# Moving four small pieces of work in a two-layer hybrid backbone: seam weights, s2 parts, last splits, context split

## The chip, the cores and the metric

One core of one Trainium2 chip runs the whole program. The metric is the time of one execution in microseconds on the device; the kernel before is given by the median of three runs. A profile was taken of one more execution. In it PE is TensorE's matmuls, PEld its weight loads, DVE is VectorE, ACT ScalarE, POOL GpSimd, and SP is SyncE, whose queue issues nearly all transfers.

## The reference

Two layers work on 1024 latent tokens and 256 context tokens of width 1024, all in float32. Only the second half of a layer matters here, the gated MLP:

```python
def conv_ffn(h, lp):
    up = h @ lp['w_up']
    gate, val = jnp.split(up, 2, axis=-1)
    gate = dwconv(gate, lp['ffn_conv_w'], lp['ffn_conv_b'], (FFN_CONV - 1) // 2)
    return (jax.nn.silu(gate) * val) @ lp['w_down']
...
    x = x + g2 * conv_ffn(modulate(rms_norm(x, lp['norm2_gain']), sh2, sc2), lp)
    if ctx_out:
        ...
        xc = xc + g2c * conv_ffn(modulate(rms_norm(xc, lp['norm2_gain']), sh2c, sc2c), lp)
```

`w_up` is 1024 x 5632 and `w_down` 2816 x 1024. `ctx_out` holds in layer 0 alone, so layer 1 has no context in its MLP.

## The kernel before, in words

**Splits.** Every float32 matmul operand is split into a rounded high part and the rest: `hi` (line 183) is a copy on ACT, `lo` (line 186) a subtraction on DVE or POOL. A product is then three matmuls, high by high, high by rest, rest by high. `weight` (line 189) loads 512 KB into a `raw` buffer (there are two), splits it on ACT and POOL, and gives a tile of the tag `wt` (there are six).

**The stages of a layer.** Phase A projects, phase B has the three head groups, `phase_c` the output projection and the MLP. In `phase_c`, `norm_ops` (line 1179) forms the operands of the up product, `up(f)` runs 22 slices of 128 columns, and each slice goes to DRAM (`ud`). `down_steps` (line 1279) takes slices 0 to 19 in five steps of four, and `down` (line 1715) takes the last two slices with weights of their own. In layer 0 that last part is a function `tail`, kept and called at the beginning of layer 1 (line 278): it stands inside a block that the framework plans as a whole with a model of time, together with phase A of layer 1. This place is called the seam.

**Seven products instead of eight.** Both big products use the Winograd form: sums of operand quarters (s1 to s4 of the activations, t1 to t4 of the weights) and seven block products. In `norm_ops` s2 = v22 - bias - v11 and s4 = v12 + bias - s2, each in four parts kk of 128 x 512; part 0 goes through a tile of its own (`sx`) and is split last. `product` (line 1546) runs kk = 0, 1, 2, 3, three matmuls each. In the last layer the order of the products of the first four slices is t1 s1, t3 s3, t4 a22, t2 s2, b22 s4. The t4 product adds into the bank of t3, after DVE has added that bank into `vb`.

**The down steps.** A step has seven products (p1 to p7), and in layer 0 a context-only factor c. `prep(g)` (line 1350) splits the two factors of product g and forms the sums of product g + 1 on POOL (`ensure`), two products ahead of use; four buffer pairs go round. `split_ctx` (line 1326) splits four context pieces of 128 x 256 on ACT and POOL; the first context product comes after the step's second product. Every product ends in DVE additions to the residual, which release its PSUM banks.

**What sets the order.** Operations are traced in the program's order, but each engine's queue is then ordered by the framework, which goes by priority and a model of when inputs are ready. So an operation that seems ready early can stand in its engine's queue in front of work that was traced before it. Inside the block of line 278 the model of time is a finer one. Engines run their queues in order.

```python
        with self.tc.block(schedule_with_timeline_sim=True):
            if l:
                self.tail()
            self.phase_a()
```

Of the kernel before, what the change touches and what calls it, by code (L numbers as in the profile page):

```python
# [11 lines left out]
F32 = mybir.dt.float32  # L12
F32R = mybir.dt.float32r
# [157 lines left out]
class Build:  # L171
# [9 lines left out]


    def hi(self, out, in_):
        self.nc.scalar.activation(out, in_, AF.Copy)  # L184

    def lo(self, out, in_, hi, eng=None):
        (eng or self.nc.vector).tensor_tensor(out, in_, hi.bitcast(F32), ALU.subtract)  # L187

    def weight(self, src, n=1024):
        nc = self.nc  # L190
# [988 lines left out]
    def norm_ops(self, xt, am, bm, accs, f_tile, bank, ops, early, outs):  # L1179
# [13 lines left out]
        def unit(name, t, c=0):  # L1193
            p = t[:, c:c + 512], t[:, c + 512:c + 1024]
            ops[name].append(p)
            return p

        def split(p, v, eng):
            self.hi(p[0], v)
            self.lo(p[1], v, p[0], eng)  # L1200
# [51 lines left out]
        for kk in range(4):  # L1252
            s3 = v21[kk]
            nc.vector.tensor_tensor(s3, v11[kk], s3, ALU.subtract)
            split(unit("s3", (wa, wb)[kk // 2], 1024 * (kk % 2)), s3, nc.vector)
        ops["s2"].append(None)
        ops["s4"].append(None)
        for kk in range(4):
# [20 lines left out]
    def down_steps(self, xt, f_tile, bank):  # L1279
# [41 lines left out]
        def load_ctx(s):  # L1321
            if not self.last:
                for i in range(4):
                    nc.sync.dma_start(ctx[i], self.ud[4 * s + i, :, NLAT:])

        def split_ctx():
            if not self.last:
                for v, (hi, lo) in zip(ctx, cs):
                    self.hi(hi, v)
                    self.lo(lo, v, hi, nc.gpsimd)  # L1330
# [19 lines left out]
        def prep(g):  # L1350
            if g >= len(seq):
                return
            s, p = seq[g]
            an, bn = ops[p][:2]
            i = g % 4
            ah, al = (t[:, :W] for t in ra[i])
            bh, bl = rb[i][:, :W], rb[i][:, W:]
            factors(g)
            if an:
                self.hi(ah, st[an])  # L1360
                self.lo(al, st[an], ah)
            self.hi(bh, st[bn])
            self.lo(bl, st[bn], bh, nc.gpsimd if g % 2 else nc.vector)
            made[s, p] = ah, al, bh, bl
            factors(g + 1)
            if s + 1 < steps:
                left = set()
                for q in [q for t, q in seq[g + 1:] if t == s]:
                    for n in ops[q][:2]:
                        left.add(n)  # L1370
                for n, (u, v, _) in sums.items():
                    if done.get(n, -1) < s:
                        left |= {u, v}
                names = [n for n in raw if n not in left and loaded[n] == s]
                for n in names:
                    loaded[n] = s + 1
                load(s + 1, *names)
# [67 lines left out]
        load_ctx(0)  # L1445
        prep(0)
        prep(1)
        split_ctx()
        if steps > 1:
            load_ctx(1)  # L1450
        g = 0
        for s in range(steps):
            mine = [p for t, p in seq if t == s]
            for i, p in enumerate(mine):
                prep(g + 2)
                g += 1
                if p != "c":
                    product(s, p)
                if not self.last:

                    for q in {1: ("p1",), len(mine) - 1: ("c",)}.get(i, ()) + ((p,) if p in ("p2", "p3") else ()):
                        context(s, q)
                if s + 1 == steps:
                    for n in {"p2": ("x12",), "p5": ("x22",), "p7": ("x21",)}.get(p, ()):
                        spread(n)
                    for n in {"p2": ("x11",), "p7": ("x22",), "p3": ("x12",), "p4": ("x21",)}.get(p, ()):
                        store(n)
            if s + 1 < steps:
                split_ctx()
                if s + 2 < steps:  # L1470
                    load_ctx(s + 2)
# [3 lines left out]
    def phase_c(self):  # L1475
# [3 lines left out]
        with ExitStack() as st:  # L1479
# [59 lines left out]
            def split(v, name, eng=None):  # L1539
                r = next(ring)  # L1540
                h, lo = r[:, 0:512], r[:, 512:1024]
                self.hi(h, v[name])
                self.lo(lo, v[name], h, eng or (nc.gpsimd if name in ("t3", "b11", "b21") else nc.vector))
                v[name] = h, lo

            def product(ps, w, a, new, wts):
                (wh, wl), aa = wts[w], ops[a]
                for kk in range(4):
                    s = slice(P * kk, P * kk + P)
                    h, lo = aa[kk]  # L1550
                    nc.tensor.matmul(ps, wh[:, s], h, start=new and kk == 0, stop=False, skip_group_check=not new)  # L1551
                    nc.tensor.matmul(ps, wh[:, s], lo, start=False, stop=False, skip_group_check=not new)  # L1552
                    nc.tensor.matmul(ps, wl[:, s], h, start=False, stop=kk == 3, skip_group_check=not new)  # L1553

            def context(ps, w, new, wts):
                hh, hl = hc
# [151 lines left out]
            def load_u(f):  # L1708
                h, lo = self.h_tile("uh"), self.h_tile("ul")
                nc.sync.dma_start(lo[:, :n_tok].bitcast(F32), self.ud[f][:, :n_tok])  # L1710
                self.hi(h[:, :n_tok], lo[:, :n_tok].bitcast(F32))
                self.lo(lo[:, :n_tok], lo[:, :n_tok].bitcast(F32), h[:, :n_tok])
                return h, lo

            def down(fs, us, ds, end=False):
# [34 lines left out]
            if self.last:  # L1750
                ds = weights()
                down([NF - 2, NF - 1], [load_u(f) for f in (NF - 2, NF - 1)], ds)
            else:
                us = []
                for f in (NF - 2, NF - 1):
                    h, lo = f_tile("uh", F32R), f_tile("ul", F32R)
                    nc.sync.dma_start(lo.bitcast(F32), self.ud[f])
                    self.hi(h, lo.bitcast(F32))
                    self.lo(lo, lo.bitcast(F32), h)
                    us.append((h, lo))  # L1760
                stack = st.pop_all()

                def tail():
                    mods, self.mods = self.mods, self.modl[l]
                    ds = weights()
                    for j in range(KC):
                        xt[j] = self.x_tile(f"xt{j}") if j < KC - 1 else self.z_tile("xt7")[:, :T]
                    for o, n in CH:
                        for j in range(KC):
                            nc.sync.dma_start(xt[j][:, o:o + n], self.xp[j][:, o:o + n])  # L1770
                    down([NF - 2, NF - 1], us, ds, True)
                    self.mods = mods
                    stack.close()
                    del self.s5

                self.tail = tail
                return
# [26 lines left out]
```

## Time and profile before

| | us |
|---|---|
| three runs | 3067.39, 3073.74, 3075.61 |
| median | 3073.74 |
| profiled execution, its own time | 3074.54 |
| its span, first to last instruction | 3072.8 |
| PE busy | 2836.2 (92%) |
| DVE busy | 2070.9 (67%) |
| POOL busy | 1520.2 (49%) |
| ACT busy | 1468.6 (48%) |

The span is the profiled execution without what lies around the first and last instruction. Layer 0 runs to about 1661, its last two down slices and layer 1 follow. A busy share is a mean over stages with different limits; the waits of PE and the timeline around them tell more.

### The profile page before, as it was taken

To read this page: it belongs to the slowest core of one execution; us is meant where nothing else is said; L and a number is where in the kernel's file an instruction comes from. 1 tells how busy PE (TensorE), PEld (TensorE's weight loads), DVE (VectorE), ACT (ScalarE), POOL (GpSimd) and SP (SyncE) were. 2 spreads that over 40 slices of the span, in tenths; PEclk is the share of its full clock that TensorE was granted. 3 is DMA by queue.
4 is the path that set the end of the run, shared out by engine and by line. 5 is a ranking of instruction groups with operands and counts; after the bars stand their busy time and mean duration, and the time that the engine had idled before them with its cause. 6 is when DMAs were issued, how large, how long until landed. Compare 5 with 4: busy or idle time off the path is not lost. (4 is left out here: it accounts for less than half of the span.)

```text
span 3072.8 us, 40965 instructions
## 1 busy us (share of the span) xinstructions
PE 2836.2 (92%) x15146; PEld 2308.8 (75%) x15146; DVE 2070.9 (67%) x2879; ACT 1468.6 (48%) x2450; POOL 1520.2 (49%) x1011
## 2 busy tenths in 40 slices
PE   6999898999899999998988899898999799999898
PEld 4798665678688888886877788666777678887776
DVE  6956656884854444457887985757885755556997
ACT  5544467784443433342332554567883444444331
POOL 4746412323554444448561765512323576665971
PEclk9999999999899999998999999999999999999999
DMA  7232627664122111143215331545533122224322
GB/s 254 83 85 82 173 61 248 185 196 172 38 81 76 67 68 67 67 182 113 83 56 192 112 109 52 145 109 168 130 121 131 55 89 83 83 83 158 123 83 83
DMA packets 208280, 349.25 MB, mean 114 GB/s; under 512 B 32720, under 2 KB 112336, under 8 KB 208080
## 3 DMA queue, kind: packets, MB, share of 16 engines
q1 hardware_dynamic: 203472, 331.69, 33.3%
q0 software_dynamic: 4608, 14.95, 2.2%
q8 instruction: 119, 1.95, 0.3%
q14 instruction: 81, 0.66, 0.1%
HBM read 257.19 MB, written 89.39 MB: 113 GB/s over the span
## 5 line engine op out<-in xcount | busy, mean ns | idle before, releaser
L184 ACT ACTIVATE w_r<-w_raw 128x512 fp32r<-128x512 f32 x338 | 212.7, 631 | 451.4 <-PE u_ps L1552 279.7
L1524 POOL TENSOR_TENSOR w_raw<-w_raw 128x512 f32<-128x512 f32 x176 | 249.9, 1425 | 229.3 <-DVE w_r L187 108.5
L187 DVE TENSOR_TENSOR w_r<-w_raw,w_r 128x512 fp32r<-128x512 f32 x206 | 151.3, 737 | 250.2 <-ACT w_r L184 250.1
L1551 PE MATMUL u_ps<-a,w_r 128*128 128x512 f32 x704 | 278.6, 396 | 5.1 <-DVE vb L1639 4.0
L1552 PE MATMUL u_ps<-a,w_r 128*128 128x512 f32 x704 | 277.5, 394 | 1.4 <-DVE a L187 1.2
L1553 PE MATMUL u_ps<-a,w_r 128*128 128x512 f32 x704 | 276.3, 392 | 0.0
L187 POOL TENSOR_TENSOR w_r<-w_raw,w_r 128x512 fp32r<-128x512 f32 x132 | 190.2, 1441 | 122.7 <-ACT w_r L184 117.5
L1403 PE MATMUL d_ps<-d_ah,d_b 128*128 128x512 f32 x560 | 225.2, 403 | 22.5 <-DVE xd L1380 12.3
L1404 PE MATMUL d_ps<-d_al,d_b 128*128 128x512 f32 x560 | 223.9, 400 | 6.2 <-DVE d_al L187 6.2
L946 DVE TENSOR_REDUCE da_sm<-da_s 128x1 f32<-128x1280 f32 (+1 forms) x144 | 194.9, 1367 | 43.6 <-PE da_s L936 42.7
L1405 PE MATMUL d_ps<-d_ah,d_b 128*128 128x512 f32 x560 | 223.3, 399 | 0.6 <-DVE d_b L187 0.6
L187 POOL TENSOR_TENSOR w<-raw,w 128x1024 fp32r<-128x1024 f32 (+2 forms) x62 | 141.1, 2283 | 144.1 <-ACT w L184 135.1
L953 ACT ACTIVATE da_e<-da_s,da_sm 128x1280 f32<-128x1280 f32 (+1 forms) x144 | 177.6, 1235 | 22.9 <-DVE da_sm L946 21.2
L1551 PEld LDWEIGHTS u_ps<-a,w_r 128*128 128x128 f32 x704 | 133.9, 190 | 34.6 <-DVE vb L1639 5.5
L1090 POOL TENSOR_TENSOR oy_x<-oy_x,oy_z 128x426 f32<-128x426 f32 (+3 forms) x48 | 52.1, 1086 | 216.3 <-ACT oy_z L1088 193.7
L1552 PEld LDWEIGHTS u_ps<-a,w_r 128*128 128x128 f32 x704 | 133.9, 190 | 29.5 <-DVE a L187 2.1
L1553 PEld LDWEIGHTS u_ps<-a,w_r 128*128 128x128 f32 x704 | 133.6, 190 | 28.8
L1380 DVE SCALAR_TENSOR_TENSOR xd<-d_ps,mods,xd 128x512 f32<-128x512 f32 x200 | 141.0, 739 | 19.7 <-PE d_ps L1405 19.4
L1403 PEld LDWEIGHTS d_ps<-d_ah,d_b 128*128 128x128 f32 x560 | 108.7, 194 | 48.3 <-DVE xd L1380 10.0
L936 PE MATMUL da_s<-dak,daq 96*128 96x512 f32 (+1 forms) x400 | 123.0, 395 | 13.7 <-ACT da_e L953 13.3
L1639 DVE TENSOR_TENSOR vb<-u_ps,vb 128x512 f32<-128x512 f32 x96 | 66.0, 688 | 99.2 <-PE u_ps L1553 90.5
L1551 PE MATMUL u_ps<-s_x,w_r 128*128 128x512 f32 x308 | 122.0, 396 | 10.1 <-ACT s_x L184 10.1
(349 smaller groups left out, 8616.3 us busy)
## 6 DMA issues: line engine op xcount, KB each, us to landing
wmod<-in_wmod SPq DMA_DIRECT2D x96, 512.0 KB, 6.5
w_raw<-in_wu SPq DMA_DIRECT2D x44, 1024.0 KB, 5.4
d_w<-in_wd SPq DMA_DIRECT2D x40, 512.0 KB, 3.9
d_a<-ud SPq DMA_DIRECT2D x40, 512.0 KB, 4.6
ud<-conv SPq DMA_DIRECT2D x22, 640.0 KB, 2.9
ud<-conv SPq DMA_DIRECT2D x22, 512.0 KB, 2.6
raw<-in_wg SPq DMA_DIRECT2D x16, 512.0 KB, 4.1
dak<-qk_da POOLq DMA_DIRECT2D x48, 160.0 KB, 4.6
```

Source lines behind the costliest of these rows:

```text
L184: self.nc.scalar.activation(out, in_, AF.Copy)
L187: (eng or self.nc.vector).tensor_tensor(out, in_, hi.bitcast(F32), ALU.subtract)
L946: nc.vector.tensor_reduce(st["sm"][:, mi:mi + 1], st["s"][mi][:, :b["nkc"]], AX.X, ALU.max, negate=True)
L953: nc.scalar.activation(e[:, :nkc], st["s"][mi][:, :nkc], AF.Exp, bias=st["sm"][:, mi:mi + 1], accum_out=b["s0"][:, ti, u["hd"], mi:mi + 1])
L1380: nc.vector.scalar_tensor_tensor(x, ps, gate, x, ALU.mult, ALU.add)
L1403: nc.tensor.matmul(ps, bh[:, w], ah[:, m], start=on is None and k == 0, stop=False, **kw)
L1404: nc.tensor.matmul(ps, bh[:, w], al[:, m], start=False, stop=False, **kw)
L1405: nc.tensor.matmul(ps, bl[:, w], ah[:, m], start=False, stop=k == 1, **kw)
L1524: sub = lambda o, a, b, op=ALU.subtract: nc.gpsimd.tensor_tensor(o, a, b, op)
L1551: nc.tensor.matmul(ps, wh[:, s], h, start=new and kk == 0, stop=False, skip_group_check=not new)
L1552: nc.tensor.matmul(ps, wh[:, s], lo, start=False, stop=False, skip_group_check=not new)
L1553: nc.tensor.matmul(ps, wl[:, s], h, start=False, stop=kk == 3, skip_group_check=not new)
```

## The change

Four pieces are moved, and nothing that is computed changes but the order of some additions.

1. `ds = weights()`, the weights of the last two down slices of layer 0, is traced before the block of layer 1 instead of in `tail`, inside it.
2. In the last layer `norm_ops` forms s2 and s4 in a new order (s2 of part 0, s4 of part 0, then s2 of 1, 2, 3 with their splits, s4 between), splits s2 before s4, and gives the low splits of parts 1 and 3 of s4 to POOL. In both layers `product` takes the parts of s2 and s4 in the order 1, 2, 3, 0.
3. The splits of the last two up slices in the last layer are each pinned behind whatever was traced before them on their engine (`keep_in_program_order`: an order only, no semaphore). For ACT that is the second weight's split, for DVE the last addition of the down steps.
4. In layer 0's down steps the first `split_ctx`, and with it the context loads of step 1, come after `prep(2)` instead of before it.

```diff
     def hi(self, out, in_):
-        self.nc.scalar.activation(out, in_, AF.Copy)
+        return self.nc.scalar.activation(out, in_, AF.Copy)
 
     def lo(self, out, in_, hi, eng=None):
-        (eng or self.nc.vector).tensor_tensor(out, in_, hi.bitcast(F32), ALU.subtract)
+        return (eng or self.nc.vector).tensor_tensor(out, in_, hi.bitcast(F32), ALU.subtract)
...
+        if self.last:
+
+            ops["s2"], ops["s4"] = [None] * 4, [None] * 4
+            raw = [(v11[kk], v12[kk]) if kk else (sx[:, 0:512], sx[:, 512:1024]) for kk in range(4)]
+
+            def s2(kk):
+                nc.vector.scalar_tensor_tensor(raw[kk][0], v22[kk], bm[:, 2 * kk, 0:1], v11[kk], ALU.subtract,
+                                               ALU.subtract)
+
+            def s4(kk):
+                nc.vector.scalar_tensor_tensor(raw[kk][1], v12[kk], bm[:, 2 * kk + 1, 0:1], raw[kk][0], ALU.add,
+                                               ALU.subtract)
+
+            def put(n, kk, eng, t=None):
+                t = t or slot()
+                ops[n][kk] = t[:, 0:512], t[:, 512:1024]
+                split(ops[n][kk], raw[kk][n == "s4"], eng)
+
+            s2(0)
+            s4(0)
+            s2(1)
+            put("s2", 1, nc.vector)
+            s2(2)
+            put("s2", 2, nc.vector)
+            s4(1)
+            s2(3)
+            put("s2", 3, nc.vector)
+            s4(2)
+            put("s2", 0, nc.vector)
+            s4(3)
+            put("s4", 1, nc.gpsimd)
+            put("s4", 2, nc.vector)
+            put("s4", 3, nc.gpsimd)
+            put("s4", 0, nc.vector, self.z_tile("s_z", F32R))
+            return None
...
         prep(0)
         prep(1)
-        split_ctx()
-        if steps > 1:
-            load_ctx(1)
         g = 0
         for s in range(steps):
             mine = [p for t, p in seq if t == s]
             for i, p in enumerate(mine):
                 prep(g + 2)
+                if g == 0:
+                    split_ctx()
+                    if steps > 1:
+                        load_ctx(1)
                 g += 1
...
-                for kk in range(4):
+
+                for i in range(4):
+                    kk = (i + 1) % 4 if a in ("s2", "s4") else i
                     s = slice(P * kk, P * kk + P)
                     h, lo = aa[kk]
-                    nc.tensor.matmul(ps, wh[:, s], h, start=new and kk == 0, stop=False, skip_group_check=not new)
+                    nc.tensor.matmul(ps, wh[:, s], h, start=new and i == 0, stop=False, skip_group_check=not new)
                     nc.tensor.matmul(ps, wh[:, s], lo, start=False, stop=False, skip_group_check=not new)
-                    nc.tensor.matmul(ps, wl[:, s], h, start=False, stop=kk == 3, skip_group_check=not new)
+                    nc.tensor.matmul(ps, wl[:, s], h, start=False, stop=i == 3, skip_group_check=not new)
...
-                self.hi(h[:, :n_tok], lo[:, :n_tok].bitcast(F32))
-                self.lo(lo[:, :n_tok], lo[:, :n_tok].bitcast(F32), h[:, :n_tok])
+
+                tc.keep_in_program_order(self.hi(h[:, :n_tok], lo[:, :n_tok].bitcast(F32)))
+                tc.keep_in_program_order(self.lo(lo[:, :n_tok], lo[:, :n_tok].bitcast(F32), h[:, :n_tok]))
...
                     us.append((h, lo))
+                ds = weights()
                 stack = st.pop_all()
 
                 def tail():
                     mods, self.mods = self.mods, self.modl[l]
-                    ds = weights()
```

## Rows read from the trace of the kernel before

**Rows 1.** The page's first part: busy time, share of the span, instructions.
```profile
PE 2836.2 (92%) x15146; PEld 2308.8 (75%) x15146; DVE 2070.9 (67%) x2879; ACT 1468.6 (48%) x2450; POOL 1520.2 (49%) x1011
```

**Rows 2.** Waits of PE, whole run: total us, times, longest us.
```profile
PE dc_ps L1425 <- DVE xd L1380: 26.3, 14, 6.7
...
PE d_ps L1403 <- DVE xd L1380: 12.3, 6, 5.9
PE u_ps L1551 <- ACT s_x L184: 10.1, 1, 10.1
...
PE d_ps L1735 <- ACT w L184: 5.9, 1, 5.9
```

**Rows 3.** Windows: length, busy of PE, PEld, DVE, ACT, POOL, granted clock, DMA share, GB/s.
```profile
1390.60:1400.80 10.20, 5.38 (x19) 4.80 (x20) 4.61 (x6) 3.23 (x4) 10.20 (x5) 0.50 0.66 206
1663.70:1670.50 6.80, 3.38 (x8) 2.65 (x9) 0.00 (x0) 2.12 (x2) 3.35 (x2) 0.50 0.97 362
2404.40:2418.00 13.60, 5.50 (x12) 4.02 (x13) 10.65 (x13) 4.14 (x7) 5.59 (x4) 0.50 0.21 78
3005.10:3011.90 6.80, 4.51 (x11) 3.55 (x12) 6.45 (x7) 4.04 (x5) 2.44 (x1) 0.50 0.04 9
41.80:712.00 670.20, 618.55 (x3744) 484.31 (x3745) 478.30 (x768) 416.01 (x783) 283.12 (x214) 0.98 0.47 136
1700.20:2311.00 610.80, 557.38 (x3455) 447.56 (x3456) 455.09 (x661) 380.96 (x680) 265.81 (x210) 0.97 0.42 118
...
3012.00:3051.00 39.00, 37.39 (x166) 30.62 (x165) 39.00 (x48) 8.99 (x9) 7.29 (x3) 1.00 0.12 39
```

**Rows 4.** Timeline of the seam, 1662 to 1676: start, us, engine, line, count, idle before.
```profile
1662.22 0.87 SPq L192 DMA_DIRECT2D raw<-in_wd  x2
1663.14 13.03 SPq L1770 DMA_DIRECT2D xt<-xp  x20
...
1667.12 2.93 PE L1735 MATMUL d_ps<-uh,w 128*128 128x512 f32 x6 [5.87 <-ACT w L184]
...
1674.94 1.41 DVE L1782 SCALAR_TENSOR_TENSOR xt<-d_ps,mods,xt 128x512 f32<-128x512 f32 x2 [12.88 <-DMA xt<-xp]
```

**Rows 5.** Timeline of the last down step and the end, layer 1.
```profile
3004.30 1.06 ACT L184 ACTIVATE uh<-ul 128x1024 fp32r<-128x1024 f32 x1 [8.11 <-DMA ul<-ud]
...
3005.45 1.23 DVE L187 TENSOR_TENSOR ul<-ul,uh 128x1024 fp32r<-128x1024 f32 x1 [5.94 <-ACT uh L184]
...
3027.39 2.41 POOL L187 TENSOR_TENSOR w<-raw,w 128x1024 fp32r<-128x1024 f32 x1 [6.00 <-ACT w L184]
...
3027.61 2.74 DVE L1380 SCALAR_TENSOR_TENSOR xd<-a,mods,xd 128x512 f32<-128x512 f32 x1
...
3041.34 0.47 PE L1403 MATMUL d_ps<-d_ah,d_b 128*128 128x512 f32 x1 [1.61 <-DVE xd L1380]
...
3045.74 5.35 DVE L1380 SCALAR_TENSOR_TENSOR xd<-d_ps,mods,xd 128x512 f32<-128x512 f32 x8
...
3068.43 0.39 PE L1737 MATMUL d_ps<-ul,w 128*128 128x512 f32 x1
```

**Rows 6.** Timeline of the last layer's first up slice, DVE and PE.
```profile
2408.62 1.75 DVE L187 TENSOR_TENSOR s_x<-xr,s_x 128x512 fp32r<-128x512 f32 x1
...
2411.08 0.80 PE L1551 MATMUL u_ps<-s_x,w_r 128*128 128x512 f32 x1 [10.13 <-ACT s_x L184]
...
2413.17 0.68 DVE L1639 TENSOR_TENSOR vb<-u_ps,vb 128x512 f32<-128x512 f32 x1
...
2423.70 0.40 PE L1551 MATMUL u_ps<-a,w_r 128*128 128x512 f32 x1
```

**Rows 7.** Timeline of layer 0's first down step, ACT and POOL.
```profile
1380.07 1.68 ACT L184 ACTIVATE d_ah<-d_a 128x1024 fp32r<-128x1024 f32 x3 [0.67 <-DMA d_a<-ud]
...
1381.51 2.95 POOL L187 TENSOR_TENSOR d_al<-d_a,d_ah 128x256 fp32r<-128x256 f32 x2 [6.25 <-PE d_ps L1405]
...
1389.23 2.34 POOL L1342 TENSOR_TENSOR d_s<-d_a,d_a 128x1024 f32<-128x1024 f32 x1
```

## The prediction

> **What bounds the kernel now.** The first part of the page comes first: PE is busy 2836.2 of 3072.8 us [rows 1]. With 92% on one engine the reader should not look for a slow operation elsewhere, but for the 237 us in which PE stands. So the view of waits follows, for PE, over the whole run [rows 2]. Four of its lines belong to the places that the diff touches: the context product behind DVE's add (26.3 us in 14 waits, the longest 6.7), the down product behind the same add (the longest 5.9), the up product behind ACT's split of `s_x` (one wait, 10.1), and the last down product of layer 0 behind the split of its weights (one wait, 5.9). The longest of each are 28.6 us together.
>
> Each stall costs more than its gap. In the four stretches around them PE runs with a granted clock of 0.50, the 1.2 GHz level, and is busy 5.38, 3.38, 5.50 and 4.51 us there [rows 3]; at the 2.4 GHz level the same matmuls would take half, so 2.7, 1.7, 2.8 and 2.3 us hang on the gaps. Everything below counts gap plus half of such a stretch.
>
> **Seam weights (part 1).** In the block of layer 1 the two 512 KB loads are issued at 1662.22, as that block's first on SP, and PE starts at 1667.12 after 5.87 us of waiting, at 1661.25 that is, for ACT's split [rows 4]. Moved ahead of the block, they queue on SP among the layer's last stores; they need a `raw` buffer, and those hold t3 and t4 until these are split. The last layer already has this order: there the two splits run on POOL inside the down steps, one 2.41 us at 3027.39 [rows 5], some 24 us before the last down add ends (3051.1). So the weights are ready, and gap and half clock go: 5.87 + 1.7 = 7.6. The residual loads also move up, from 1663.14 to about 1662.2 [rows 4]. Given back: POOL's two splits now fall on a DVE that has little spare time. One DVE add that reads SBUF twice took 2.74 us beside such a split [rows 5], against 5.35/8 = 0.67 for the adds from PSUM; in the last layer PE lost 1.61 us to it [rows 5]. I take that price: 7.6 - 1.6 = **6**. The best is 7.6. The worst is below nothing: if the first residual add stays at 1674.94 [rows 4], PE fills its six banks (36 matmuls of 37.39/166 = 0.225 us [rows 3], 8.1 us) by 1669.4 and stops until 1675.6, where before it had these 36 done by about 1677.0; that leaves 1.4, less two such DVE delays of 2.0: -2.6.
>
> The Trainium skill has a rule that speaks against this part (SBUF — State Buffer, Who interferes with whom): a DVE instruction with two SBUF inputs and a GpSimd instruction that reads SBUF exclude one another for the whole instruction. The 2.74 us agree in kind; by the rule each split could cost DVE all of its 2.4 us, 4.8 instead of 1.6, and the kernel would end some 3 us later than the sum below.
>
> **s2 first (part 2).** After the s3 products PE waits 10.13 us, then runs the product of s2 with t2 [rows 6]. Two things hold it: s2's part 0 is split last but read first, and t4's product cannot go before DVE has added the t3 bank into `vb` at 2413.17, behind all of the s2/s4 work [rows 6]. DVE's own work hardly changes: the same eight subtractions, six low splits instead of seven (less 0.6 us), one more on POOL, which can lengthen a DVE operation beside it by about 1.1 (1.75 against 0.68 [rows 6]). So DVE still frees PE at about 2414.4. What changes is what is then left for PE: parts 1 to 3 of s2 are there earlier, so s2's 12 matmuls run inside the wait, and 24 remain, 5.4 us: 2419.8 instead of 2423.70 for the next product [rows 6], a gain of **4**. Between 0 (PE's order stays as it is and stops at its third matmul) and 6.6 (the add comes early too and only the 12 of s4 remain). In layer 0 only the order within the product changes; its up phase has no such wait, since the 10.1 us are one wait [rows 2]. The two returned values, `hi` and `lo`, add no instruction.
>
> **Last splits (part 3).** ACT's split of `uh` at 3004.30 stood 8.11 us waiting for its load in front of four other splits, and DVE's at 3005.45 stood 5.94 in front of an add that PE needed [rows 5]. Pinned, ACT's two go behind the second weight split, where its queue is empty, and DVE's two behind its last down add. From there DVE is full: 39.00 of 39.00 us between 3012 and 3051 [rows 3]. It gains the idle 5.94 and passes two splits of 1.1 on to the end: 8.2, the same as PE's 5.9 + 2.3. But the end pays. Now the last add ends at 3045.74 + 5.35 = 3051.1 and PE is done 17.7 later, at 3068.8 [rows 5]. Afterwards PE's third matmul of a bank needs `ul`, 1.2 us behind that add. With six banks, 12 of the 96 matmuls can run before; the other 84 take 18.9, so PE ends 20.2 behind the add, 2.5 later; with one bank open, 4.7 later. Taken: 8.2 - 2.5, rounded down for the one-bank case, **5**. Between 0 (another load wait takes the place) and 7.1 (1.61 more [rows 5]).
>
> **Context split (part 4).** POOL idles 6.25 us in front of the second pair of context splits at 1381.51, then forms t2, t4 and only at 1389.23 s1, whose split DVE needs before the adds that release PE's bank [rows 7]. Moved behind the third preparation, t2 and t4 (two sums, 4.8 us) come first and fit into that idle time. s1 then waits for a22, which ACT reads at 1380.07 [rows 7]: 9.2 us earlier at most, 4.8 less if the second context pair still goes first. PE can get back 6.7 + 2.7 = 9.4. The four context loads of step 1 also move on SP, behind those of `prep(2)`; their first use is a step later, tens of us away. Taken: **5**, near the lower end, because POOL is full right after (10.20 of 10.20 us [rows 3]) and may pass on only part. Between 0 (order unchanged) and 9.2.
>
> **Sum.** 6 + 4 + 5 + 5 = 20 us from the profiled execution's 3074.54 (span 3072.8 and 1.7 around it): 3054.5. The median of the runs is 0.8 below that execution, so 3054.
>
> **Rivals.** *DVE is the bound* (0.14): in parts 2 and 3 the freed time meets an engine that is full. For it: 39.00 of 39.00 [rows 3]. Against: the 5.94 us are DVE's own idle time. Then parts 2 and 3 give 0 and part 1 pays 3.5: 4 + 5 = 9, 3065.
>
> *The moves do not take* (0.12): the order on an engine is a planner's, not the program's; the program's very last splits ran in the middle of the down steps [rows 5]. Nothing is pinned in parts 2 and 4, so they may stay: 6 + 5 = 11, 3063. Against: whatever is traced earlier goes first where two are ready.
>
> *The layer-1 block is planned worse* (0.12), the one on the slow side. Two loads and four splits leave the block that is planned as a whole, and everything in it may be reordered. Its place is 1700.2 to 2311, where PE stands 610.8 - 557.4 = 53.4 us [rows 3]. It must grow to over 82 us to eat the 20 and another 9: 3084. Against: the same work in layer 0, planned apart, stands 670.2 - 618.6 = 51.6 [rows 3], so two plans differ by 2 us, not 30.
>
> **How the numbers follow.** The forecast has 0.62, with 3041 to 3064 (parts at their upper ends 30 us, hardly all at once). About 0.3%, 9.2 us, is what a measurement can tell from no change, as the three runs lie within 8.2. The second rival lies at that bound and is halved: faster 0.62 + 0.06 = 0.68, same 0.14 + 0.06 = 0.20, slower 0.12. The range goes from 3041 to 3074: part 1 below nothing and the rest at 0 reach 3076, and beyond it are the last rival and a few hundredths below.
>
> **What would show it.** Part 1: no load of `in_wd` at the head of SP's block, PE's wait before L1735 under 1 us, ACT's `w` splits before 1650. Part 2: the wait before the first `s_x` matmul under 5 us and 12 of them in a row; if three come alone, the second rival. Part 3: `uh` behind both `w` splits, no wait over 2 us after 2999, a new one of 1 to 3 us in front of an L1737. Part 4: POOL forms t2 before the second context pair, s1 by 1385, and the 6.7 us shrink below 3. It is wrong if PE's idle time in the layer-1 block moves by more than 10 us, or if these stalls go and others of the same size stand behind them.

## The result, and the profile after

The changed kernel is slower by 0.9%, which is clear of the noise: 3097.57 us (median of four runs, 3096.25 to 3101.04) against 3071.0 us for the kernel before (four runs, 3067.39 to 3075.61). The ratio is 1.0087, 95% interval 1.0069 to 1.0106. The forecast was 3054, with 3041 to 3074.

The changed file is longer, so lines move: the matmuls of the down steps are L1438 to L1440 (L1403 to L1405 before), the context product L1460, the up product L1589 to L1591, the last two slices L1774 to L1776 (L1735 to L1737), the residual additions L1415 and L1821. The page's first part, beside [rows 1]:

```profile
PE 2838.0 (92%) x15146; PEld 2302.3 (74%) x15146; DVE 2052.5 (66%) x2878; ACT 1469.8 (47%) x2449; POOL 1504.2 (49%) x1012
```

PE does the same matmuls in nearly the same busy time, 1.8 us more. The span grew by 26.5 us, so the rest is time in which PE stands. The waits of PE over the whole run, beside [rows 2]:

```profile
PE dc_ps L1460 <- DVE xd L1415: 22.8, 15, 4.4
...
PE sw_s L866 <- ACT tr L614: 17.0, 2, 16.9
...
PE qkv_ps L636 <- ACT w L184: 11.2, 3, 9.4
...
PE qkv_ps L636 <- DVE xt L1821: 6.4, 1, 6.4
PE gate_ps L578 <- issue: 6.0, 2, 5.6
...
PE u_ps L1589 <- ACT s_x L184: 4.9, 2, 3.7
```

The waits that the change aimed at are gone or shorter: the seam's (5.9) is not in the list, the up product's went from 10.1 to 3.7, the context product's longest from 6.7 to 4.4. New ones of 16.9, 9.4 and 5.6 us stand in phase A of layer 1, which no line of the diff touches. The windows say how much it is. They cut the run at the end of the down steps, at the first projection (`qkv_ps`) and just ahead of the first matmul of the sliding-window attention (`sw_s`) of layer 1, and at the first sum of its output projection (columns as in [rows 3]). The stretch from the first projection to `sw_s` is called phase A, and the one behind it phase B. Before:

```profile
1661.20:1700.20 39.00, 30.76 (x157) 26.28 (x157) 22.87 (x41) 15.93 (x24) 13.61 (x8) 0.91 0.85 306
1700.20:1981.00 280.80, 262.29 (x1242) 222.32 (x1242) 217.84 (x283) 140.97 (x208) 180.22 (x104) 0.96 0.34 93
1981.00:2310.10 329.10, 294.18 (x2208) 224.49 (x2209) 236.75 (x378) 239.15 (x472) 84.97 (x105) 0.97 0.49 140
```

After:

```profile
1654.70:1690.20 35.50, 29.12 (x159) 25.12 (x157) 26.27 (x44) 15.83 (x25) 12.72 (x8) 0.98 0.94 323
1690.20:2007.80 317.60, 268.60 (x1242) 222.61 (x1242) 200.48 (x282) 141.14 (x204) 158.75 (x102) 0.92 0.30 82
2007.80:2340.90 333.10, 297.49 (x2208) 227.43 (x2209) 238.25 (x376) 239.19 (x470) 83.65 (x105) 0.96 0.47 137
...
1970.00:2008.00 38.00, 14.18 (x31) 5.85 (x30) 21.09 (x19) 22.92 (x27) 10.79 (x5) 0.71 0.37 89
```

The 1242 matmuls of phase A take 317.6 us instead of 280.8: 36.8 us more. PE's idle time in them goes from 18.5 to 49.0 us, and the busy time rises by 6.3, at a mean granted clock of 0.92 instead of 0.96; in the last 38 us it is 0.71. The account of the profiled executions, with the end of layer 0 at -6.5 us: seam -3.5, phase A +36.8, phase B up to the output projection +4.0 (3.3 of it busy time), all that follows -4.3: +26.5.

What happens in phase A is seen in the order of PE's queue. First the timeline of PE in the kernel before, then after:

```profile
1725.65 0.35 PE L427 MATMUL cx_ps<-n,w 128*128 128x428 f32 x1
...
1884.39 0.36 PE L427 MATMUL cx_ps<-n,w 128*128 128x428 f32 x1
...
1959.17 0.28 PE L638 MATMUL qkv_ps<-w,n 128*128 128x256 f32 x1
...
1981.46 0.51 PE L866 MATMUL sw_s<-swk,swq 128*128 128x256 f32 x2 [0.47 <-ACT tr L614]
```

```profile
1690.18 0.77 PE L636 MATMUL qkv_ps<-w,n 128*128 128x512 f32 x1 [6.38 <-DVE xt L1821]
...
1725.39 1.22 PE L636 MATMUL qkv_ps<-w,n 128*128 128x512 f32 x2 [9.36 <-ACT w L184]
...
1763.73 0.42 PE L427 MATMUL cx_ps<-n,w 128*128 128x428 f32 x1
...
1942.02 0.28 PE L638 MATMUL qkv_ps<-w,n 128*128 128x256 f32 x1
...
1942.49 0.45 PE L427 MATMUL cx_ps<-n,w 128*128 128x428 f32 x1
...
1981.50 3.18 PE L578 MATMUL gate_ps<-xc,lw 128*128 128x428 f32 x4 [5.56 <-issue]
...
2007.85 0.80 PE L866 MATMUL sw_s<-swk,swq 128*128 128x256 f32 x2 [16.86 <-ACT tr L614]
```

`cx_ps` is the product that begins a recurrence group (its weight is called the convolution weight below): its result goes through a convolution, gates and two scans on DVE, three groups one after the other. In the queue of before the first `cx_ps` stands behind 96 projection matmuls, after the change behind 240: 25.4 us behind the first projection before (1725.65 less 1700.22), 73.6 after. The third group ends in the longest single wait. Before, its `cx_ps` begins at 1884.39, and projections for PE run until 1959.45, beside its gates and scans. After, it begins at 1942.49, behind the very last projection. From there on PE has little to do but follow the chain (14.18 us of work in the last 38), whose end is seen on DVE and ACT:

```profile
2001.85 2.35 DVE L599 TENSOR_TENSOR_SCAN tr<-av,tr,ti 128x1024 f32<-128x1024 f32 x1
...
2006.71 1.08 ACT L614 ACTIVATE tr<-cg_ps 128x512 f32<-128x512 f32 x2 [8.88 <-POOL tr L608]
```

The last scan ends at 2004.2 (at 1964.3 before), POOL adds the two directions, ACT writes `tr`, and 0.1 us behind it `sw_s` may begin. The 9.36 us at 1725.39 are another effect of the new order: ACT's split of the fourth projection weight stands behind the norm's operations.

```profile
1705.80 1.06 ACT L184 ACTIVATE w<-raw 128x1024 fp32r<-128x1024 f32 x1 [4.15 <-PE n_col L392]
...
1724.28 1.06 ACT L184 ACTIVATE w<-raw 128x1024 fp32r<-128x1024 f32 x1 [1.79 <-POOL n L187]
```

Its load was issued at about 1689. So what part 1 takes out of the block changes the order of what remains in it. That was the theory ("plan"); the rival was that the early loads and splits, or parts 2 to 4, cost the time by themselves ("own cost").

### The profile page after: what moved, and what is told of

The parts are those of the page before. It is cut to its first block, busy times and chain, and to the rows that moved or that the text cites. A ratio compares the mean times of both kernels' runs of the same rounds, so it can differ in the third digit from the quotient of the medians.

```text
span 3099.3 us, 40983 instructions
## 1 busy us (share of the span) xinstructions
PE 2838.0 (92%) x15146; PEld 2302.3 (74%) x15146; DVE 2052.5 (66%) x2878; ACT 1469.8 (47%) x2449; POOL 1504.2 (49%) x1012
## 5 line engine op out<-in xcount | busy, mean ns | idle before, releaser
L1589 PE MATMUL u_ps<-a,w_r 128*128 128x512 f32 x704 | 279.8, 398 | 4.5 <-DVE vb L1677 4.4
L1591 PE MATMUL u_ps<-a,w_r 128*128 128x512 f32 x704 | 277.7, 394 | 0.0
L1438 PE MATMUL d_ps<-d_ah,d_b 128*128 128x512 f32 x560 | 222.7, 399 | 19.2 <-DVE a L1447 11.9
L1440 PE MATMUL d_ps<-d_ah,d_b 128*128 128x512 f32 x560 | 221.8, 396 | 0.0
L1589 PEld LDWEIGHTS u_ps<-a,w_r 128*128 128x128 f32 x704 | 134.6, 191 | 34.7 <-DVE vb L1677 6.3
L1591 PEld LDWEIGHTS u_ps<-a,w_r 128*128 128x128 f32 x704 | 134.1, 191 | 29.2
L1415 DVE SCALAR_TENSOR_TENSOR xd<-d_ps,mods,xd 128x512 f32<-128x512 f32 x200 | 141.1, 740 | 20.1 <-PE d_ps L1440 20.0
L1438 PEld LDWEIGHTS d_ps<-d_ah,d_b 128*128 128x128 f32 x560 | 107.2, 192 | 44.8 <-issue 7.8
L936 PE MATMUL da_s<-dak,daq 96*128 96x512 f32 (+1 forms) x400 | 122.8, 395 | 14.1 <-ACT da_e L953 13.9
L1439 PEld LDWEIGHTS d_ps<-d_al,d_b 128*128 128x128 f32 x560 | 107.6, 192 | 31.3 <-DVE d_al L187 9.6
```

The costliest lines, as they stand in the source:

```text
L1415: nc.vector.scalar_tensor_tensor(x, ps, gate, x, ALU.mult, ALU.add)
L1438: nc.tensor.matmul(ps, bh[:, w], ah[:, m], start=on is None and k == 0, stop=False, **kw)
L1439: nc.tensor.matmul(ps, bh[:, w], al[:, m], start=False, stop=False, **kw)
L1440: nc.tensor.matmul(ps, bl[:, w], ah[:, m], start=False, stop=k == 1, **kw)
L1589: nc.tensor.matmul(ps, wh[:, s], h, start=new and i == 0, stop=False, skip_group_check=not new)
L1591: nc.tensor.matmul(ps, wl[:, s], h, start=False, stop=i == 3, skip_group_check=not new)
```

## Experiments

One table first. The queue column counts the projection matmuls ahead of the first `cx_ps` in PE's queue; the third group's `cx_ps` is "covered" when it begins 73 us or more ahead of the end of the last projection, "uncovered" when it begins behind it. The stretch is from the end of layer 0's last down step to the first `sw_s` of layer 1, in the profiled execution. Each ratio is to runs of the kernel before that were taken beside it (their medians lie between 3071.0 and 3076.36), so ratios are compared here, and times only with their own neighbours.

| kernel | projections ahead of first cx_ps | third group | stretch, us | ratio, 95% interval |
|---|---|---|---|---|
| before | 96 | covered | 320.2 | 1 |
| changed | 240 | uncovered | 353.0 | 1.0087 (1.0069 to 1.0106) |
| e1_no_part1 | 96 | covered | 320.4 | 0.9964 (0.9952 to 0.9977) |
| e2_only_part1 | 240 | uncovered | 355.1 | 1.0137 (1.0122 to 1.0153) |
| e3_tail_outside | 96 | covered | 331.8 | 1.0034 (1.0021 to 1.0046) |
| e4_wx_first | 20 | uncovered | 355.4 | 1.0080 (1.0067 to 1.0092) |
| e5_third_group_first | 240 | covered | 347.5 | 1.0045 (1.0030 to 1.0060) |
| e6_all_groups_first | 20 | covered | 325.7 | 0.9974 (0.9961 to 0.9987) |
| e7_one_weight_early | 121 | covered | 323.1 | 0.9977 (0.9968 to 0.9986) |
| e8_late_without_part1 | 240 | uncovered | 348.8 | 1.0091 (1.0077 to 1.0105) |
| e9_groups_two_three | 240 | covered | 342.9 | 1.0044 (1.0030 to 1.0057) |
| e10_raw_early | 123 | covered | 323.4 | 0.9979 (0.9970 to 0.9988) |
| e11_raw_early_pool | 123 | covered | 323.7 | 0.9976 (0.9965 to 0.9987) |
| e12_no_part1_pool | 96 | covered | 320.4 | 0.9951 (0.9937 to 0.9964) |

**Part 1 undone, and part 1 alone.**

```diff
-                ds = weights()
                 stack = st.pop_all()
 
                 def tail():
                     mods, self.mods = self.mods, self.modl[l]
+                    ds = weights()
```

> The changed kernel with part 1 undone (the seam weights are loaded inside the block again); parts 2, 3 and 4 stay. Theory 'plan': part 1 alone gave the layer-1 block another order, with the convolution products of the recurrence (cx_ps) behind 240 projection matmuls instead of 96; undone, the block runs in the order of before, and what is left is the sum of the other parts by the two traces, -6.5 (part 4), -1.4 (part 2), -4.7 (part 3), so about 12.5 us below the kernel before: 3058, ratio 0.996. Theory 'own cost': parts 2 to 4 or their side effects (the later context loads, the extra POOL splits, a queue held by a pin) lose the time; then this kernel stays at 3085 to 3097. PE should wait for ACT's split of the seam weights again, 5 to 6 us.

> The kernel before with part 1 alone. Theory 'plan': seam stall of 5.9 us gone, but the block in the other order: from the two traces the offset between changed kernel and before goes from -6.5 at the end of layer 0 to +30.8 at the output projection of layer 1, so +37: 3108, ratio 1.012, with a PE wait of 15 to 20 us in front of the first sw_s matmul. Theory 'own cost' (of parts 2 to 4): 3064 to 3074, ratio at or below 1.0, no such wait.

Measured: 3063.82 us without part 1 and 3114.47 with part 1 alone, beside 3074.17. Both ratios are near where "plan" put them (0.996 and 1.012; the second came out somewhat above). In phase A the 1242 matmuls of PE write the same tiles in the same order as before in the one, and as in the changed kernel in the other. Waits of PE with part 1 alone, then without it:

```profile
PE sw_s L866 <- ACT tr L614: 17.0, 2, 16.9
...
PE qkv_ps L636 <- ACT w L184: 11.0, 3, 9.1
```

```profile
PE d_ps L1774 <- ACT w L184: 6.2, 1, 6.2
```

So parts 2 to 4 together gain some 11 us, and part 1 turns that into a loss. This still leaves open whether the order costs or something else that comes with early weights.

**The order of the changed kernel without part 1.** The kernel before, edited in `phase_a`: in groups one and three of layer 1 all ten projection tiles are traced ahead of the recurrence, and its first matmul is pinned there.

```diff
-                pipe = self.qkv(grp, ws, n, range(4), hh, hl, psp) if j == 0 else []
+                late = l and j in (0, 2)
+                pipe = self.qkv(grp, ws, n, range(10 if late else 4), hh, hl, psp) if j == 0 else []
+                if late and j:
+                    pipe = self.qkv(grp, ws, n, range(10), hh, hl, psp)
+                self.pin = late
...
-                tiles = list(range(4 if j == 0 else 0, 10))
+                tiles = [] if late else list(range(4 if j == 0 else 0, 10))
...
+            if f and getattr(self, 'pin', False):
+                self.tc.keep_in_program_order(m)
+                self.pin = False
```

> The kernel before (none of the four parts), with the order of the changed kernel's phase A imposed by hand in layer 1: the first and the third group's convolution are traced behind all ten projection tiles and pinned there; the seam weights stay inside the block. If the place of these convolutions is the cause, it must be slow without part 1: ratio 1.008 to 1.014, 3095 to 3115, with gates and scan of the third group behind the last projection and a PE wait of 10 to 20 us ahead of the first sw_s matmul. If the early loads of part 1 do it in another way (buffers, queues, POOL), this kernel stays within 10 us of before: ratio 1.000 to 1.003.

Measured: 3102.71 us, 1.0091. Waits of PE: the long one ahead of `sw_s` is back, with the seam weights where they were before.

```profile
PE sw_s L873 <- ACT tr L621: 18.0, 2, 17.9
PE qkv_ps L643 <- DVE qb L692: 17.0, 4, 14.4
...
PE d_ps L1742 <- ACT w L184: 6.2, 1, 6.2
```

The late place of the recurrence is enough by itself to bring the wait back; early weights are not needed for it, and in that the rival falls. Of the size it shows a part only. This kernel has none of the gains of parts 2 to 4, so the one to compare with is part 1 alone, at 1.0137. Counted to `sw_s` itself, phase A takes 281.2 us before, 319.6 with part 1 alone and 309.7 here, so 28.5 of 38.4 us are reproduced. The 14.4 us for `qb` are a wait of this kernel's own, as the changed kernel waits at most 4.6 us there: the imposed order is not the changed kernel's in all its places. Its phase A:

```profile
1699.40:2009.10 309.70, 263.46 (x1242) 219.31 (x1242) 207.36 (x284) 143.30 (x209) 168.73 (x104) 0.92 0.31 85
```

**Early weights, recurrence early.** Four kernels move one or more groups of the changed kernel forward, by tracing a group's convolution weight ahead of its four projection weights; for the third group (`if l:` for second and third; in the first group the lines that load `ws` and `wx` change places):

```diff
                 if j:
+                    if l and j == 2:
+                        wx = self.weight(self.a["wc"][l, j])
                     ws = [self.qkv_weight(grp, kk) for kk in range(4)]
...
```

> The changed kernel with the convolution weight of the first recurrence group traced ahead of the four projection weights of layer 1. In its order the first group's convolution stands behind 20 projection matmuls (96 before, 240 in the changed kernel), the second and third group as late as in the changed kernel. If the lateness of the first group is what costs (the three groups being one chain from there on), it comes to 3055 to 3065. If it is the last group, whose chain has no projections left behind it to cover it, it stays at 3090 to 3100 with the 15 to 20 us wait in front of sw_s.

> The changed kernel with one edit: in layer 1 the convolution weight of the third recurrence group is traced ahead of that group's four projection weights. Its order on TensorE is that of the changed kernel up to the third group; there the convolution now stands ahead of nearly all projections instead of behind them. Theory 'last group': the loss sits in the chain of the third group (convolution, gates, scan) that ends with nothing left for TensorE; covered by the projections again, the 16.9 us wait in front of sw_s, the 5.6 and 1.4 in front of its gates and their half clock go: about 24 us back, 3070 to 3076, ratio 0.998 to 1.003. Theory 'whole order' (the late first group, the 9.4 us wait for the fourth projection weight and the worse mixture of the rest): at most 8 us back, 3089 to 3097.

> The changed kernel with the convolution weight traced ahead of the projection weights in the second and third group of layer 1; the first group stays as late as in the changed kernel (behind 240 projection matmuls), and the 9.4 us wait for the fourth projection weight stays. So far: first group alone 1.0080, third alone 1.0045, all three 0.9974, changed kernel 1.0087. If the three groups are one serial chain on the engines behind PE, a late first group keeps most of the loss and this is at 1.002 to 1.0045. If only the end of phase A counts, it comes within 9 us of the kernel with all three: 0.998 to 1.0005.

> The changed kernel with the convolution weight traced ahead of the four projection weights in all three groups of layer 1: seam weights early and every recurrence chain early. If the block's order is all that part 1 lost, this has the gains of all four parts: the kernel without part 1 was at 0.9964, and the seam's 7.6 less the 4 us that the first projection waits more for the residual come on top: 3055 to 3062, ratio 0.994 to 0.9965. If the early weights cost something by themselves (a longer wait for the residual, POOL's splits), it ends above 3064.

Measured: first group alone 3099.02, nothing gained, its wait ahead of `sw_s` still 16.8; third alone 3090.68; second and third 3087.67, no more than the third alone; all three 3066.39. The expectation for the third alone missed on both sides: it gained 1.0087 less 1.0045, some 13 us of the 24, and by the traces only 6.4 of them in phase A (317.7 to 311.3, counted to `sw_s`). The wait ahead of `sw_s` went, but 9.1 us for the fourth weight stayed, as the waits of that kernel show, and DVE's work behind the projections (L698) now ends last at the end of the phase:

```profile
PE qk_t L703 <- DVE qa L698: 22.0, 12, 5.1
...
PE qkv_ps L640 <- ACT w L184: 12.2, 4, 9.1
...
PE sw_s L870 <- ACT sw_p L882: 5.4, 3, 2.8
```

The windows of phase A in the kernel with groups two and three early, and in that with all three:

```profile
1688.30:1995.70 307.40, 271.62 (x1242) 225.25 (x1242) 203.86 (x281) 140.96 (x205) 165.96 (x102) 0.92 0.32 85
```

```profile
1687.40:1978.00 290.60, 266.69 (x1243) 224.18 (x1243) 210.64 (x282) 140.73 (x205) 169.75 (x102) 0.94 0.34 90
```

The first group makes 16.8 us between these two, but alone it made none: it helps only where the end is covered too. So no single group is the cause. With all three early the seam weights stay early, phase A is 27.0 us shorter than in the changed kernel and the kernel is at 0.9974: most of the loss was the order. It missed its 0.994 to 0.9965, and by the sign named ahead (above 3064, the 0.9965 of its range) this counts as a cost of the early weights. Phase A is still 9.8 us longer than before (290.6 against 280.8), which takes the seam's gain. Whether these 9.8 us are the weights' own cost or what is left of the other order, no run separates.

**The seam without the block, and other ways to load early.**

```diff
+        if l:
+            self.tail()
         with self.tc.block(schedule_with_timeline_sim=True):
-            if l:
-                self.tail()
             self.phase_a()
```

> The changed kernel with the whole seam (tail) traced ahead of the block, so that the planned block holds phase A alone; the weights are as early as in the changed kernel. Theory 'plan': the convolution products stand behind 96 projection matmuls again, so phase A is as fast as before: 3071 - 12.5 - 7.6 = 3051, up to 3058 if the seam without the finer plan loses some us; ratio 0.993 to 0.996. Theory 'own cost' of the early loads and splits (buffers held, POOL and SP busy): 3090 to 3100, since they are where the changed kernel has them.

Measured: 3084.56, between the theories; my 3051 to 3058 left out what the seam costs when it is not planned with phase A. Its windows (seam, phase A) and the seam's longest wait:

```profile
1653.80:1715.60 61.80, 35.47 (x174) 29.94 (x173) 48.89 (x84) 33.23 (x59) 20.13 (x18) 0.77 0.59 191
1715.60:1985.60 270.00, 255.67 (x1225) 216.07 (x1225) 193.16 (x239) 121.33 (x170) 163.77 (x91) 0.98 0.34 93
...
1706.53 0.98 PE L392 MATMUL n_col<-one,sqs 128*128 128x1 f32 x4 [13.98 <-DVE sqs L390]
```

Phase A is 10.8 us shorter than before (17 of its matmuls now stand in the seam), but the seam is 22.8 longer: PE waits 14 us there for the squares of the norm, and its clock is 0.77.

The next two keep the seam in the block: one loads only the first weight ahead of it, one loads both raw weights ahead into a wide buffer and splits them inside.

```diff
-                ds = weights()
+                raw2 = self.wt_tile("raw_s", F32)
+                raws = [raw2[:, 0:1024], raw2[:, 1024:2048]]
+                for raw, f in zip(raws, (NF - 2, NF - 1)):
+                    nc.sync.dma_start(raw, self.a["wd"][l, f])
...
```

> The changed kernel with only the first of the two seam weights loaded ahead of the block, the second at its head. In its order the first convolution stands behind 121 projection matmuls and the third ahead of its projections, nearly as before. Theory 'plan': no long wait in front of sw_s; the seam still waits for the second weight, some 4 us instead of 5.9, so 1 to 3 us below the kernel without part 1: 3059 to 3064, ratio 0.995 to 0.9965. If an early weight costs by itself: above 3070.

> The changed kernel with the two seam loads ahead of the block, into a wide weight buffer, but their splits inside it. In its order the first convolution stands behind 123 projection matmuls, the third ahead of its projections, as in the kernel with one early weight. If the plan decides, no long wait ahead of sw_s, and the seam waits for two splits (1.1 us each) and not for the loads: 2 to 5 us below the kernel without part 1 (0.9964), so 0.995 to 0.9965. If its plan costs as much as the one-weight kernel's (0.9977), 0.997.

Measured: 3067.85 and 3068.39, no long wait ahead of `sw_s` in either, 0.9977 and 0.9979 where 0.995 to 0.9965 was expected (for the second the other case that it names, 0.997, is nearer). Each has an order of its own, with a phase A of 288.7 and 292.1 us against 280.8. In the second the seam takes 31.2 us instead of 39.0, which is as much as the 7.6 that part 1 was to bring, and phase A takes it back. That is four ways to have the weights early (e3, e6, e10, and one of the two in e7), and none is measurably below the kernel without part 1.

**The rests of the last slices on POOL** (on top of e10, then on top of e1):

```diff
-                tc.keep_in_program_order(self.lo(lo[:, :n_tok], lo[:, :n_tok].bitcast(F32), h[:, :n_tok]))
+                tc.keep_in_program_order(self.lo(lo[:, :n_tok], lo[:, :n_tok].bitcast(F32), h[:, :n_tok], nc.gpsimd))
```

> As the kernel with the two seam loads ahead of the block and their splits inside, with one more edit on part 3: the rests of the last two up slices are split on POOL, behind its last weight split, instead of on DVE behind its last down addition. The ledger of the kernel without part 1 shows 3.7 us given back where PE waits for DVE's ul splits. If POOL forms them while DVE adds, 2 to 4 us less than the kernel without this edit, seen as no wait ahead of the first matmul with ul. If POOL's split (2.4 us each, beginning after its last weight split) comes later than DVE's, 0 to 3 us more.

> The changed kernel with part 1 undone and the rests of the last two up slices split on POOL instead of DVE. The block keeps the order of before (-7.5 by parts 2 to 4 as in the kernel without part 1: ratio 0.9964) and the 3.7 us given back at the end, where PE waits for DVE's ul splits, do not appear (they did not in the kernel with early loads and POOL's split): 3060, ratio 0.9945 to 0.996, the best so far. If POOL's split only moves the wait, 0.9955 to 0.997.

Measured: 3067.9 and 3059.33. The first missed its 2 to 4 us: it is 0.5 below e10 (3068.39), within the noise. The second lies in its range. In the second kernel POOL is done some 10 us before PE needs `ul`, and the wait for it is gone; a wait of 1.8 us for a DVE addition stands further ahead. POOL's and PE's timeline of that kernel:

```profile
3023.51 2.85 POOL L187 TENSOR_TENSOR ul<-ul,uh 128x1024 fp32r<-128x1024 f32 x1
...
3030.18 0.47 PE L1438 MATMUL d_ps<-d_ah,d_b 128*128 128x512 f32 x1 [1.82 <-DVE xd L1415]
...
3036.17 0.39 PE L1776 MATMUL d_ps<-ul,w 128*128 128x512 f32 x1
```

The last stretch, 72.9 us before (2995.94 to 3068.82), takes 68.2 us here and 70.3 without this edit; in the pair with early loads 67.3 and 68.2. The kernel without part 1 and with this edit is the fastest of all, 0.9951 (0.9937 to 0.9964), clearly below before and changed kernel; the intervals of the two kernels without part 1 overlap, so what the POOL edit adds is not settled.

## Why the prediction was wrong

**The forecast's sum was of stalls removed, and most of them were.** By the traces:

*Part 1* gained its 5.87 and the half clock, 7.6 as put: layer 0 ends 6.4 us earlier than before, and twelve matmuls into the seam PE is 14.1 us earlier (1657.48 against 1671.54). But 4.0 came back at the seam's end, not 1.6: the first projection waits 6.38 us for DVE's residual instead of 2.39. The term also had the wrong reason. POOL's two splits, which the 1.6 stood for, begin at 1626.96 and 1635.66 and are done by 1639.1, some 50 us before. What the residual addition at 1689.57 stands behind on DVE is an operation of the norm, which before came behind the last additions:

```profile
1687.20 2.44 DVE L418 SCALAR_TENSOR_TENSOR n<-tms,mods,n 128x512 fp32r<-128x512 f32 x1
```

In e10, whose splits stay in the block, the projection waits 2.40 us as before and the seam keeps 7.8. So this loss, too, goes with the order of the block. The seam's net is 3.5 (39.0 to 35.5), inside the bounds.

*Part 2* gained 1.4 us instead of 4: the stretch around it, 77.6 us before (2386.27 to 2463.85), takes 76.2. In the other kernels with part 2 it is 1.2 to 1.9 us shorter (0.1 in one), in the two without it 0.0 and 0.1. PE's timeline of the changed kernel:

```profile
2431.92 0.50 PE L1589 MATMUL u_ps<-s_x,w_r 128*128 128x512 f32 x1 [1.13 <-ACT s_x L184]
2433.14 0.79 PE L1590 MATMUL u_ps<-s_x,w_r 128*128 128x512 f32 x1 [0.71 <-DVE s_x L187]
2437.65 0.80 PE L1589 MATMUL u_ps<-s_x,w_r 128*128 128x512 f32 x1 [3.73 <-ACT s_x L184]
...
2448.23 0.39 PE L1589 MATMUL u_ps<-a,w_r 128*128 128x512 f32 x1
...
2455.99 0.50 PE L1591 MATMUL u_ps<-s_x,w_r 128*128 128x512 f32 x1 [1.66 <-DVE w_r L187]
```

The step that s2's 12 matmuls run inside the wait failed: two run, the third stands until ACT has split another part. The case "PE's order stops at its third matmul" was in the text as the lower bound. Yet the product behind, at 2423.70 before and at 2448.23 here, begins 5.3 us earlier (both counted from the matmul at 2386.27, here 2416.13), more than the 4 forecast. DVE's addition into `vb`, which the sum left in its place, came 4.4 us earlier, so there two errors offset each other, which is luck. The gain did not last. The split of the weights that PE needs there (`w_r`, on DVE) is only 1.8 us earlier than before, and PE, which is 5.3 earlier, now waits 1.66 us for it, up to 2455.99. With the slower clock behind (0.78 from 2452.7 to 2460.3) that gives back 3.9. So the step that cost the forecast its gain is that it was counted at the next product and taken to last. What stood behind is the first rival, "DVE is the bound".

*Part 3* gained 2.0 to 4.7 us over the last 72.9 us in the kernels that have it as written (5 forecast). The new wait behind DVE's last addition is there as foretold, 1 to 3 us ahead of the matmul with `ul`. DVE and PE of the changed kernel:

```profile
3074.24 2.35 DVE L187 TENSOR_TENSOR ul<-ul,uh 128x1024 fp32r<-128x1024 f32 x2
...
3075.51 0.50 PE L1776 MATMUL d_ps<-ul,w 128*128 128x512 f32 x1 [1.72 <-DVE ul L187]
```

*Part 4* gained 5.2 to 7.5 us from the first matmul of the down steps to the thousandth, in all kernels that have it (5 forecast). The wait fell to 4.44, not below 3. POOL and PE of the changed kernel, beside [rows 7]:

```profile
1382.14 3.02 POOL L187 TENSOR_TENSOR d_al<-d_a,d_ah 128x256 fp32r<-128x256 f32 x2 [1.34 <-ACT d_ah L184]
...
1387.46 2.38 POOL L1377 TENSOR_TENSOR d_s<-d_a,d_a 128x1024 f32<-128x1024 f32 x1
...
1393.69 0.58 PE L1460 MATMUL dc_ps<-d_ah,d_b 128*128 128x256 f32 x1 [4.44 <-DVE xd L1415]
```

POOL's 6.25 us of idle time in front of the second context pair are 1.34 now, but s1 comes only 1.8 us earlier (2.5 counted from the first down matmul), less than the 4.4 of the case in which that pair still goes first. So the size came out and the way to it only in part. In the changed kernel, 4.6 us are gained in the first 300 matmuls, and 2.7 in the next 300, where the waits are those of before. Windows of 294 matmuls there, before and after; PE has four waits in each, of 5.9 and of 6.0 us together:

```profile
1448.20:1513.30 65.10, 59.17 (x294) 49.94 (x294) 54.48 (x63) 18.83 (x21) 40.79 (x20) 0.95 0.27 83
```

```profile
1444.30:1506.70 62.40, 56.34 (x294) 47.17 (x294) 55.01 (x63) 18.72 (x21) 40.74 (x20) 1.00 0.28 87
```

The waits are the same, but the granted clock is 1.00 instead of 0.95, and the busy time 2.8 us less. The sum had no term for that.

**What decided was the third rival**, "the layer-1 block is planned worse", which had 0.12 and 3084. The step that failed is the sentence against it: that the same work in layer 0, planned apart, stands 51.6 us, "so two plans differ by 2 us, not 30". Those were two plans of one kind. In layer 0, too, the first `cx_ps` stands behind 96 projections, so the pair said nothing of a plan that puts it elsewhere. What had to be asked is what in the block is a long chain (the recurrence, three groups in a row) and what covers it (projections that can stand beside it), and that could be read from the trace of before. In the sum itself this cost stood at nothing. The rival's threshold held: in the stretch that it named, phases A and B (only A lies in the block), PE stands 49.0 + 35.6 = 84.6 us now, over the 82. Its price was low, since it counted idle time alone, while everywhere else the prediction counted stalls with their half clock: PE's busy time in the stretch rose by 9.6 us too (268.6 + 297.5 against 262.3 + 294.2). By the windows the stretch lost 36.8 + 4.0 = 40.8 us, and the rest gained 6.5 + 3.5 + 4.3 = 14.3 where 20 were forecast: 26.5 more, which on the 3071.0 of the runs is the 3097.5 that was measured.

What stays open is why the planner puts the recurrence so late when the seam's splits are not in its block. The traces show the orders that it gives (20 to 240 projections ahead), not its reasons.

## What to carry to other kernels

Work that is moved across the edge of a region planned as a whole changes the plan of everything left inside, and this can outweigh what the move was for: here 3.5 us gained at the seam, 36.8 lost in a phase without an edited line. Before such a move, look for the longest dependent chain in the region and for the independent work that covers its last link, compare the queues of both kernels, and let this case have a chance of its own size, with stalls priced at idle time plus the slower clock that follows. Parts of a change whose gains add up elsewhere are best kept apart from such a move: parts 2 to 4 without it are 0.9964, and 0.9951 with the last rests on POOL.

## What the runs showed of the hardware

A part of what a wait costs or gives back does not show in the list of waits. In the two windows of part 4 above, PE has the same 294 matmuls and 5.9 and 6.0 us of waits, but is busy 59.17 us at a granted clock of 0.95 and 56.34 at 1.00.

A mean granted clock does not tell this cost by itself, since the mean takes in the time in which PE stands. For the same 1242 matmuls of phase A, PE was busy 262.3 us at a mean of 0.96 before. At a mean of 0.92 it was busy 268.6 us in the changed kernel, 271.6 with groups two and three early, and only 263.5 with the late order imposed. So the busy time itself is what to compare: 6.3 of the 36.8 us lost in the changed kernel, and 9.3 of 26.6 in the kernel whose longest wait is 9.3 us.
